# An encoder layer on one core: thirteen of the second matrix's sixteen pairs in seven products, the rest block by block, and the projection in one group

## The chip, the cores and the metric

The kernel runs on one core of a Trainium2 chip, as one program. The metric is the device time in microseconds (us) from the program's start to its end; lower is better. The kernel before takes 2405.2 us, the median of three runs that lie between 2405.2 and 2405.23 us.

## What is computed

One layer of an encoder is applied to two groups of tokens with the same weights: a prompt of 512 tokens and a sample of 1024 tokens, both with 1024 features. In short:

```
h = LN(x) * (1 + scale1) + shift1
x = LN1(alpha * x + gate1 * (m @ w_out))        # m: what two branches (convolution, long convolution) give
h = LN(x) * (1 + scale2) + shift2
f = square(relu(h @ mlp_w1 + mlp_b1))           # mlp_w1: 1024 x 4096
x = LN2(alpha * x + gate2 * (f @ mlp_w2 + mlp_b2))   # mlp_w2: 4096 x 1024
```

All of it is float32. The change concerns the sample's second half: the projection with `w_out`, and the two products of the MLP.

## The kernel before

**Products.** A float32 product is made of three matmuls of a reduced format (`mm3`, line 223): both operands are split into a high and a low part (`split`, line 201: ScalarE copies the high part, VectorE subtracts it from the source), and high by high, high by low and low by high are added up in PSUM. A weight tile of 128x512 therefore costs one DMA of 256 KB, one ScalarE copy and one VectorE subtraction before TensorE can use it.

**Order.** A tile scheduler lays down a fixed order of instructions for each engine; `soon(n)` moves what is issued within it n places of priority ahead. All DMAs stand in one queue, that of SP, and are issued in its order: a DMA whose buffer is not free yet holds up those behind it. All matmuls write PSUM tiles named `mm`, `fx` and `tr`, which hold 128x512 each; at most eight of them are in use.

**Projection (`w_out_ln1`, line 1018).** The sample's tokens are two blocks of 512, `tb` = 0 and 1, with four rows of 128 tokens each. A loop over four column quarters loads and splits four weight tiles (`wpiece`) and multiplies them for the rows of a group, in 128x256 products. For `tb` = 0 both pairs of rows form one group; for `tb` = 1 they are two groups one after the other, and each loads all 16 weight tiles anew. After a group's last quarter its rows are normalised (`ln1_pair`) in pieces that later steps pull from `self.todo`.

**First MLP matrix (`up_seven`, line 1263).** The 1024x1024 blocks of `h` and of each of 16 pairs of weight columns are multiplied with Strassen's scheme in Winograd's form: seven products in place of eight, of 12 matmuls each. Only some of the operands need the second token block. For the first `NE` = 12 pairs an early loop therefore does products 1 and 2 and parks what the main loop needs of them in DRAM (`d_xs`, `d_p`); `h2_second` (line 989), pulled one step at a time, makes the operands of the others. The main loop then does five products for an early pair and seven for a late one. Its results go to DRAM in seven slots of `d_p`, which hold the left operands of the second matrix: among them the sums `s1`, `s2`, `s4` and the difference `p21 - p11`, which only the seven products need.

**Second MLP matrix (`down_seven`, line 1396).** Again 16 pairs in seven products, here in four passes over the pairs, because the accumulators of one or two products fill PSUM: pass 1 (slots 0 and 1), pass 2 (slots 2 and 3), pass 3 (slots 4 and 5) and pass 4 (slot 6). Each step of a pass loads weights of 512 KB into a `pg` row (pass 2 one more of 256 KB into a `raw` tile, line 1464), forms weight sums on VectorE where the scheme needs them (`raw` and `pg`, line 1465 on), splits them into `wt` tiles, and loads and splits 512 KB of left operands (`load_p`, line 1427). A step is 24 matmuls of 128x512. The four double pairs that pass 4 does last are held back and done row by row (`held`), so that each row of `tb` = 0 can be finished by `ln2_end` (line 1534) while the next is multiplied. Those of `tb` = 1 are finished during pass 4 by `ln2_block` (line 1107).

Of the kernel before, what the change touches and what calls it, by code (L numbers as in the profile page):

```python
# [38 lines left out]
HD = 90  # L39
NE = 12  # L40
NL = 8
# [120 lines left out]
class Enc:  # L162
# [855 lines left out]
    def w_out_ln1(self, g):  # L1018
# [244 lines left out]
    def up_seven(self, g):  # L1263
# [4 lines left out]

        nc, v = self.nc, self.V
# [12 lines left out]
        for n in range(NE):  # L1282
# [25 lines left out]
        for n in range(NP):  # L1308
# [13 lines left out]
            def finish(last):  # L1322
# [7 lines left out]
                s4 = self.sg()  # L1330
                v.tensor_tensor(s4, t, s2, op=ALU.subtract)
                put(n - 1, 6, s4)
# [63 lines left out]
    def down_seven(self, g):  # L1396


        nc, v = self.nc, self.V
        w2 = self.a["mlp_w2"]  # L1400
        NP = 16
        row = lambda: self.pg(F32, (128, 2, 512))
# [4 lines left out]
        acc, st = {}, {}  # L1407
# [7 lines left out]
        def both(src, wt=True):  # L1415

            new = (lambda: self.p_wt.tile([128, 2, 512], F32R, tag="wt", name="wt")) if wt else self.pg
            h, l = new(), new()
            self.split(src, h, l)
            return h, l  # L1420

        def products(ps, p, w, j, i, first, last, more, blocks=range(4)):
            for m in blocks:
                k = slice(128 * m, 128 * m + 128)
                self.mm3(ps[m], p[0][:, j, k], p[1][:, j, k], w[0][:, i], w[1][:, i], first, last, skip_group_check=more)

        def load_p(src):
            t = row()
            nc.sync.dma_start(t, src)
            return both(t, False)  # L1430

        def half(t, tb, m, h):

            cs = slice(512 * h, 512 * h + 512)
            v.tensor_tensor(t, t, gate[:, cs], op=ALU.mult)
            v.tensor_tensor(acc[tb, m][:, cs], acc[tb, m][:, cs], t, op=ALU.add)
# [4 lines left out]
        for n in range(NP):  # L1441
            with self.soon(HD):
                t = row()
                nc.sync.dma_start(t, w2[2 * n:2 * n + 2, :, 0:512].rearrange("f p c -> p f c"))
                w = both(t)
                p = load_p(g.d_p[n, :, 0:2])
            products(b, p, w, 1, 1, n == 0, n == NP - 1, False)
            products(a, p, w, 0, 0, n == 0, n == NP - 1, False)
            if n % 2 and todo:
# [6 lines left out]
        for m in range(4):  # L1456
            v.tensor_tensor(ts[m], a[m], ts[m], op=ALU.add)
        t2 = {}
        for n in range(NP):
            with self.soon(HD):  # L1460
                t = row()
# [6 lines left out]
                v.tensor_tensor(u, u, t[:, 1], op=ALU.subtract)  # L1468
                v.tensor_tensor(s, t[:, 0], u, op=ALU.add)
                w6, w7 = self.piece(s), self.piece(u)  # L1470
                p = load_p(g.d_p[n, :, 2:4])
            products(b, p, (w7[:, 0:1], w7[:, 1:2]), 1, 0, n == 0, n == NP - 1, False)
            products(a, p, (w6[:, 0:1], w6[:, 1:2]), 0, 0, False, n == NP - 1, True)
            if n < 4:
                half(ts[n], 0, n, 0)
                st[n] = self.p_xt.tile([128, 2, 6], F32, tag="st2", name="st2")
                v.bn_stats(st[n][:, 0], acc[0, n][:, 0:512])
            yield 5.2
        m7, us = [], []
# [6 lines left out]
        for n in range(NP):  # L1486
            with self.soon(HD):
                t = row()
# [3 lines left out]
                w = both(t)  # L1492
# [9 lines left out]
        held = []  # L1502
        for n in range(0, NP, 2):
            late = n >= NP - NL
            with self.soon(HD):
                t = row()
                nc.sync.dma_start(t, w2[2 * n + 1:2 * n + 4:2, :, 512:1024].rearrange("f p c -> p f c"))
                w = both(t, n < NP - 2)
                p = load_p(g.d_p[n:n + 2, :, 6].rearrange("f p c -> p f c"))
            if n // 2 < 4:  # L1510
                m = n // 2
                half(m7[m], 1, m, 1)
                half(us[m], 1, m, 0)
                self.todo.append([self.ln2_block(g, 1, m, acc[1, m], lg, lb), 0])
            if late:
                held.append((p, w))
                continue
            for j in range(2):
                products(a, p, w, j, j, False, False, True)
            yield 5.2  # L1520
        for m in range(4):
            for k, (p, w) in enumerate(held):
                for j in range(2):
                    products(a, p, w, j, j, False, k == len(held) - 1 and j == 1, True, [m])
                yield 1.3
            t = self.so()
            v.tensor_tensor(t, a[m], gate[:, 512:1024], op=ALU.mult)
            s = acc[0, m]
            v.tensor_tensor(s[:, 512:1024], s[:, 512:1024], t, op=ALU.add)
            v.bn_stats(st[m][:, 1], s[:, 512:1024])  # L1530
            self.todo.append([self.ln2_end(g, m, s, st[m], lg, lb), 0])
        self.flush()

    def ln2_end(self, g, m, s, st, lg, lb):
        v = self.V
        mv = self.sm([128, 1, 2], tag="mv")
        v.bn_aggr(mv[:, 0], st)
        r = self.rstd(mv, 1)
        yield
        v.scalar_tensor_tensor(s, s, mv[:, 0, 0:1], lg, op0=ALU.subtract, op1=ALU.mult)  # L1540
        v.scalar_tensor_tensor(s, s, r[:, 0:1], lb, op0=ALU.mult, op1=ALU.add)
        yield
# [243 lines left out]
```

## Time and profile before

| what | value |
| --- | --- |
| median of three runs | 2405.2 us |
| the profiled execution's own time | 2408.34 us |
| its span | 2406.6 us |
| granted TensorE clock, mean | 0.988 |
| DMA, mean over the span | 175 GB/s |
| HBM read, written | 323.76 MB, 96.27 MB |

The profile shows one execution. Durations are those of its instructions; a stage's cost is read from a window of the trace: how long the stage lasts, how long each engine is busy in it, and what the engine that matters waits for. TensorE is named PE in the rows, VectorE DVE, ScalarE ACT, and the queue of SP is SPq. Instructions that a helper records all carry that helper's line (L145, L202), so tiles tell them apart better than lines do: in the second matrix `wt` is a split weight, `pg` a left operand or a row of the output, `raw` a weight as loaded; `st`, `mv` and `sm` belong to a normalisation.

### The profile page before, as it was taken

The numbers are of one execution on the slowest core, as the hardware profiler recorded it, in microseconds if no ns is written. First come the engines' busy times: TensorE is split into PE (matmuls) and PEld (weight loads), VectorE is DVE, ScalarE is ACT, GpSimd is POOL, SyncE is SP. The second block draws the span as 40 slices with busy tenths as digits, with TensorE's granted clock in tenths as the row PEclk, the third lists the DMA queues.
The fourth block names the chain that finished last, engine by engine and source line by source line (L and its number), as shares of the span: only waits on it lengthen the run. The fifth ranks groups of instructions, "written<-read, shape, count | busy, mean of one in ns | idle before, by whom it ended". The sixth has DMA issues, their size and how long they took to land.

```text
span 2406.6 us, 33012 instructions
## 1 busy us (share of the span) xinstructions
PE 2276.9 (95%) x11648; PEld 1878.9 (78%) x11648; DVE 1896.9 (79%) x3618; ACT 931.9 (39%) x1507; POOL 54.1 (2%) x149
## 2 busy tenths in 40 slices
PE   6999999999999999899999999997999999987995
PEld 3878777878878888888888887897777787866873
DVE  5988797877989989876988867749887785555678
ACT  3464422422222223365442353223664454423431
POOL 2110100000000000000000000000000000000000
PEclk9999999999999999999999999999999999999997
DMA  6555436663465566633433255545776666746543
GB/s 240 182 167 173 147 93 201 202 216 127 155 205 176 176 223 222 203 99 125 139 119 116 91 193 173 173 136 164 244 231 210 205 202 222 255 140 219 179 153 122
DMA packets 198250, 422.22 MB, mean 175 GB/s; under 512 B 22809, under 2 KB 33227, under 8 KB 197573
## 3 DMA queue, kind: packets, MB, share of 16 engines
q1 hardware_dynamic: 197253, 419.10, 52.7%
q8 instruction: 92, 1.51, 0.3%
q0 software_dynamic: 832, 1.02, 0.2%
q14 instruction: 73, 0.60, 0.1%
HBM read 323.76 MB, written 96.27 MB: 175 GB/s over the span
## 4 chain that ended last, share of the span: by engine, by line
PE 52%; DVE 13%; DMA 9%; issue 3%; ACT 2%; SPq 1%; DVEq 0%; ACTq 0%
PE mm L145 37%; PE fx L145 13%; DVE pg L145 3%; DVE wt L145 2%; PE tr L145 2%; DMA sg<-d_xs 1%; DVE fp L145 1%; DVE sg L145 1%; DVE st L145 1%; DMA sg<-ks 1%; DMA pg<-in_mlp_w_dram 1%; DMA raw<-in_w_out_dram 1%; DMA fp<-in_w_ada_dram 1%; DMA fp<-in_dec_s_dram 1%; DVE sm L145 1%
## 5 line engine op out<-in xcount | busy, mean ns | idle before, releaser
L145 PE MATMUL mm<-pg,wt 128*128 128x512 f32 (+1 forms) x4776 | 1139.9, 391 | 7.9 <-DVE xt L145 4.0
L145 PEld LDWEIGHTS mm<-pg,wt 128*128 128x128 f32 x4776 | 878.2, 189 | 196.9 <-issue 11.9
L145 PE MATMUL mm<-wt,pg 128*128 128x512 f32 (+1 forms) x2640 | 509.3, 348 | 22.8 <-DVE pg L145 14.1
L145 PEld LDWEIGHTS mm<-wt,pg 128*128 128x128 f32 x2640 | 422.3, 191 | 91.7 <-DVE pg L145 18.0
L202 ACT ACTIVATE wt<-raw 128x512 fp32r<-128x512 f32 x422 | 263.3, 629 | 455.4 <-PE mm L145 356.0
L145 DVE TENSOR_TENSOR wt<-raw,wt 128x512 fp32r<-128x512 f32 x422 | 284.6, 685 | 71.5 <-ACT wt L202 69.1
L145 DVE SCALAR_TENSOR_TENSOR cv<-cv,pp 128x512 f32<-128x512 f32 (+1 forms) x288 | 288.8, 1010 | 7.7 <-ACT cv L853 2.7
L145 PEld LDWEIGHTS fx<-fp,fft 128*128 128x128 f32 x1536 | 177.5, 192 | 22.7 <-issue 14.7
L145 PE MATMUL fx<-fp,fft 128*128 128x128 f32 x1536 | 184.2, 277 | 4.0 <-DVE fp L145 1.8
L145 DVE TENSOR_TENSOR fp<-fp 128x256 f32<-128x256 f32 (+2 forms) x328 | 145.1, 481 | 15.9 <-ACT fp L380 10.1
L145 DVE TENSOR_TENSOR sg<-fx,sg 128x512 f32<-128x512 f32 (+1 forms) x162 | 98.6, 630 | 47.7 <-PE fx L145 30.6
L145 PE MATMUL fx<-wt,pg 128*128 128x512 f32 x432 | 114.6, 403 | 19.7 <-ACT pg L202 18.4
L202 ACT ACTIVATE wt<-pg 128x1024 fp32r<-128x1024 f32 (+1 forms) x55 | 51.5, 936 | 193.4 <-DVE pg L145 84.7
L145 DVE TENSOR_TENSOR pg<-so,pg 128x512 fp32r<-128x512 f32 (+1 forms) x147 | 89.9, 617 | 37.7 <-ACT pg L202 26.4
L145 PEld LDWEIGHTS fx<-wt,pg 128*128 128x128 f32 x432 | 81.6, 192 | 42.7 <-ACT pg L202 22.6
L145 DVE TENSOR_TENSOR wt<-pg,wt 128x1024 fp32r<-128x1024 f32 (+1 forms) x55 | 58.8, 1068 | 68.5 <-ACT wt L202 68.4
L145 DVE TENSOR_TENSOR pg<-pg,pg 128x1024 fp32r<-128x1024 f32 (+1 forms) x74 | 88.9, 1220 | 10.0 <-DMA pg<-in_mlp_b_dram 6.6
L1260 ACT ACTIVATE so<-so,pp 128x512 f32<-128x512 f32 x60 | 43.2, 720 | 129.2 <-DVE so L145 128.9
L145 PE MATMUL fx<-pg,pg 128*128 128x512 f32 x384 | 92.8, 389 | 0.0
L202 ACT ACTIVATE pg<-so 128x512 fp32r<-128x512 f32 (+1 forms) x112 | 62.9, 567 | 68.9 <-DVE so L145 52.1
L145 DVE TENSOR_TENSOR sg<-sg 128x256 f32<-128x256 f32 (+2 forms) x187 | 82.2, 460 | 5.0 <-ACT sg L890 3.8
L145 PEld LDWEIGHTS fx<-pg,pg 128*128 128x128 f32 x384 | 72.0, 188 | 15.1 <-DVE so L145 0.2
(171 smaller groups left out, 2217.5 us busy)
## 6 DMA issues: line engine op xcount, KB each, us to landing
raw<-in_mlp_w_dram SPq DMA_DIRECT2D x188, 256.0 KB
raw<-in_w_in_dram SPq DMA_DIRECT2D x144, 256.0 KB
pg<-in_mlp_w_dram SPq DMA_DIRECT2D x56, 512.0 KB
pg<-d_p SPq DMA_DIRECT2D x56, 512.0 KB
fp<-in_w_ada_dram SPq DMA_DIRECT2D x48, 512.0 KB
raw<-in_w_out_dram SPq DMA_DIRECT2D x80, 256.0 KB
d_p<-so SPq DMA_DIRECT2D x64, 256.0 KB
d_g<-so SPq DMA_DIRECT2D x48, 256.0 KB
```

The lines of the kernel that those rows point to most:

```text
L145: return f(*args, **kw)
L202: self.nc.scalar.activation(hi, src, AF.Copy)
L1260: nc.scalar.activation(out, src, AF.Relu, bias=self.pp[:, C_B1 + f:C_B1 + f + 1], scale=1.0)
```

## The change

In the projection the rows of `tb` = 1 form one group, as those of `tb` = 0 do. In the first matrix 14 pairs are early instead of 12; the steps of `h2_second` are pulled from pair 8 on, behind a flush of the pending normalisation; and the last three pairs don't make `s1`, `s2`, `s4` and the difference. In the second matrix the first 13 pairs (`N7`) go through the seven products and the last three are multiplied block by block. Pass 3 becomes two passes of one product each (`single`), pass 4 a third of them. Weights are loaded in quarters of 256 KB, by turns into `raw` and `xr` tiles, and no longer in 512 KB rows of `pg`. For the last three pairs the weights are multiplied by the gate before they are split, and every row of 128 tokens gets its 36 matmuls directly and then its normalisation by `ln2_block`; `ln2_end` and `held` are gone.

```diff
-NE = 12
-NL = 8
+NE = 14
+N7 = 13
...
-            groups = [[0, 2]] if tb < g.nb - 1 else [[0], [2]]
+            groups = [[0, 2]] if g.nb > 1 else [[0], [2]]
...
-                if not self.todo:
+                if n >= NE - 6:
+                    if n == NE - 6 and k == 1:
+                        self.flush()
                     next(sums, None)
...
-            s1, s2 = self.sg(), self.sg()
-            v.tensor_tensor(s1, p21, p22, op=ALU.add)
-            put(n, 4, s1)
-            v.tensor_tensor(p21, p11, p21, op=ALU.subtract)
+            s2 = None
+            if n < N7:
+                s1, s2 = self.sg(), self.sg()
+                v.tensor_tensor(s1, p21, p22, op=ALU.add)
+                put(n, 4, s1)
+                v.tensor_tensor(p21, p11, p21, op=ALU.subtract)
+                v.tensor_tensor(s2, s1, p11, op=ALU.subtract)
+                put(n, 2, s2)
             put(n, 3, p21)
-            v.tensor_tensor(s2, s1, p11, op=ALU.subtract)
-            put(n, 2, s2)
...
+        def quarter(f, h):
+            t = self.xt("xr") if count[0] % 2 else self.p_raw.tile([128, 512], F32, tag="raw", name="raw")
+            count[0] += 1
+            nc.sync.dma_start(t, w2[f, :, 512 * h:512 * h + 512])
+            return t
...
-        for n in range(NP):
+        for n in range(N7):
             with self.soon(HD):
-                t = row()
-                nc.sync.dma_start(t, w2[2 * n].rearrange("p (h c) -> p h c", h=2))
-                u = self.p_raw.tile([128, 512], F32, tag="raw", name="raw")
-                nc.sync.dma_start(u, w2[2 * n + 1, :, 512:1024])
+                b11, b12, b22 = quarter(2 * n, 0), quarter(2 * n, 1), quarter(2 * n + 1, 1)
...
-        for n in range(NP):
-            with self.soon(HD):
-                t = row()
-                nc.sync.dma_start(t, w2[2 * n + 1].rearrange("p (h c) -> p h c", h=2))
-                s = t2[n // 2][:, n % 2:n % 2 + 1]
-                v.tensor_tensor(t, t, s.to_broadcast([128, 2, 512]), op=ALU.subtract)
-                w = both(t)
-                p = load_p(g.d_p[n, :, 4:6])
-            order = [(b, 1, 0), (a, 0, 1)]
-            for ps, j, i in order if n < NP - 1 else order[::-1]:
-                products(ps, p, w, j, i, False, n == NP - 1, True)
-            yield 5.2
+        def single(acc_ps, slot, row, h, minus, ops):
+            for n in range(0, N7, 2):
+                js = range(min(2, N7 - n))
+                with self.soon(HD):
+                    w = []
+                    for j in js:
+                        t = quarter(2 * (n + j) + row, h)
+                        if minus:
+                            v.tensor_tensor(t, t, t2[n // 2][:, j], op=ALU.subtract)
+                        w.append(self.piece(t))
...
+                for j in js:
+                    products(acc_ps, p, w[j], j, False, n + j == end, True)
+                some(ops, 2)
+                yield 5.2
...
+        yield from single(a, 4, 1, 1, True, iter(()))
         for m in range(4):
             v.tensor_tensor(m7[m], a[m], m7[m], op=ALU.add)
+        yield from single(b, 5, 1, 0, True, chain(*[half(m7[m], 1, m, 1) for m in range(4)]))
...
+        def rest_w(f, h, k):
+            t = quarter(f, h)
+            v.tensor_tensor(t, t, gate[:, 512 * h:512 * h + 512], op=ALU.mult)
+            wl[f, h] = w = self.pg(first=True) if k < 9 else self.p_wt.tile([128, 2, 512], F32R, tag="wt", name="wt")
+            self.split(t, w[:, 0], w[:, 1])
+
+        def rest_p(f, tb):
+            t = self.so()
+            nc.sync.dma_start(t, g.d_p[f // 2, :, (0, 1, 3, 5)[2 * tb + f % 2]])
+            x = pl[f, tb] = self.pg()
+            self.split(t, x[:, 0], x[:, 1])
...
+        last = single(a, 6, 1, 1, False, chain(*[half(us[m], 1, m, 0) for m in range(4)]))
+        for us_ in last:
+            with self.soon(HD):
+                some(prep, 2)
+            yield us_
...
+        for tb in (1, 0):
+            for m in range(4):
...
+                for h in range(2):
+                    ps = self.fx_ps() if m % 2 else self.mm_ps()
+                    for i, f in enumerate(fs):
+                        x, w = pl[f, tb], wl[f, h]
+                        self.mm3(ps, x[:, 0, k], x[:, 1, k], w[:, 0], w[:, 1], i == 0, i == len(fs) - 1)
+                    d = s[:, 512 * h:512 * h + 512]
+                    v.tensor_tensor(d, d, ps, op=ALU.add)
+                    yield 2.6
+                self.todo.append([self.ln2_block(g, tb, m, s, lg, lb), 0])
         self.flush()
```

How the change moves instructions is shown at two places. The first is SP's queue in pass 2 of the second matrix. In the kernel before, `pg2_19740`, `19787`, `19833` and `19880` are the 512 KB weight rows of the pass's pairs 0, 1, 2 and 3, `raw_19928`, `19971`, `20013` and `20056` the 256 KB quarters of pairs 4 to 7, and the loads from `d_p` the left operands of pairs 0 to 3:

```order
L1462 DMA pg2_19740<-in_mlp_w2_dram 128x1024
L1429 DMA pg2_19753<-d_p1_95 128x1024
L1462 DMA pg2_19787<-in_mlp_w2_dram 128x1024
L1429 DMA pg2_19799<-d_p1_95 128x1024
L1464 DMA raw_19928<-in_mlp_w2_dram 128x512
L1462 DMA pg2_19833<-in_mlp_w2_dram 128x1024
L1429 DMA pg2_19846<-d_p1_95 128x1024
L1464 DMA raw_19971<-in_mlp_w2_dram 128x512
L1462 DMA pg2_19880<-in_mlp_w2_dram 128x1024
L1429 DMA pg2_19892<-d_p1_95 128x1024
L1464 DMA raw_20013<-in_mlp_w2_dram 128x512
L1464 DMA raw_20056<-in_mlp_w2_dram 128x512
```

In the changed kernel's pass 2, `pg2_19702`, `19747` and `19793` are the left operands of pairs 2, 3 and 4; `raw_19869` and `raw_19873` with `xr_19871` are the three weight quarters of pair 6, `xr_19915`, `raw_19917` and `xr_19919` those of pair 7, and `raw_19960` and `raw_19964` belong to pair 8:

```order
L1418 DMA raw_19869<-in_mlp_w2_dram 128x512
L1418 DMA raw_19873<-in_mlp_w2_dram 128x512
L1429 DMA pg2_19702<-d_p1_95 128x1024
L1418 DMA xr_19871<-in_mlp_w2_dram 128x512
L1418 DMA xr_19915<-in_mlp_w2_dram 128x512
L1418 DMA xr_19919<-in_mlp_w2_dram 128x512
L1429 DMA pg2_19747<-d_p1_95 128x1024
L1418 DMA raw_19917<-in_mlp_w2_dram 128x512
L1418 DMA raw_19960<-in_mlp_w2_dram 128x512
L1429 DMA pg2_19793<-d_p1_95 128x1024
```

Before, a pair's 512 KB weight row stands right ahead of its left operands; now all of a pair's weight quarters stand some four pairs ahead of the left operands.

The second place is the end of VectorE's work, where `st` and `mv` are a row's statistics, `sm` the small steps to its scale, and the two SCALAR_TENSOR_TENSOR with `mv` and with `sm` its normalisation. Before, from the last row's statistics to the program's end:

```order
L145 BN_AGGR mv<-st_19924 128x2
L145 TENSOR_SCALAR sm<-sm 128x1
L145 SCALAR_TENSOR_TENSOR pg<-pg,mv,pg_19110 128x1024
L145 TENSOR_SCALAR sm<-sm 128x1 x5
L145 TENSOR_SCALAR sm<-mv 128x1
L145 SCALAR_TENSOR_TENSOR pg<-pg,sm,pg_19112 128x1024
L145 TENSOR_SCALAR sm<-sm 128x1 x8
L145 TENSOR_SCALAR sm<-mv 128x1
L145 SCALAR_TENSOR_TENSOR pg<-pg,sm,pg_19112 128x1024
L145 TENSOR_SCALAR sm<-sm 128x1 x8
L145 SCALAR_TENSOR_TENSOR pg<-pg,sm,pg_19112 128x1024
```

In the changed kernel, from the last product that is added (`fx`) to the end:

```order
L145 SCALAR_TENSOR_TENSOR pg<-pg,sm,pg_19024 128x1024
L145 TENSOR_TENSOR pg<-pg,fx 128x512
L145 BN_STATS st<-pg 128x6
L145 BN_AGGR mv<-st 128x2
L145 TENSOR_SCALAR sm<-mv 128x1
L145 SCALAR_TENSOR_TENSOR pg<-pg,mv,pg_19022 128x1024
L145 TENSOR_SCALAR sm<-sm 128x1 x8
L145 SCALAR_TENSOR_TENSOR pg<-pg,sm,pg_19024 128x1024
```

Before, three rows are still to be normalised when the last one's statistics are done; now the row ahead is finished before the last product is added.

More of the change, by code (lines that the diff above doesn't have):

```diff
@@ L1413, in base, with load_p, products, some @@
             v.scalar_tensor_tensor(s, s, ALPHA, gb, op0=ALU.mult, op1=ALU.add)
[L1415 to L1419, printed above, removed]
+        def load_p(src):
+            t = self.pg(F32, (128, 2, 512))
+            nc.sync.dma_start(t, src)
+            h, l = self.pg(), self.pg()
+            self.split(t, h, l)
             return h, l
-        def products(ps, p, w, j, i, first, last, more, blocks=range(4)):
-            for m in blocks:
+        def products(ps, p, w, j, first, last, more):
+            for m in range(4):
                 k = slice(128 * m, 128 * m + 128)
-                self.mm3(ps[m], p[0][:, j, k], p[1][:, j, k], w[0][:, i], w[1][:, i], first, last, skip_group_check=more)
-        def load_p(src):
-            t = row()
-            nc.sync.dma_start(t, src)
-            return both(t, False)
+                self.mm3(ps[m], p[0][:, j, k], p[1][:, j, k], w[:, 0], w[:, 1], first, last, skip_group_check=more)
         def half(t, tb, m, h):
             cs = slice(512 * h, 512 * h + 512)
-            v.tensor_tensor(t, t, gate[:, cs], op=ALU.mult)
-            v.tensor_tensor(acc[tb, m][:, cs], acc[tb, m][:, cs], t, op=ALU.add)
+            d = acc[tb, m][:, cs]
+            yield v.tensor_tensor(t, t, gate[:, cs], op=ALU.mult)
+            yield v.tensor_tensor(d, d, t, op=ALU.add)
+        def some(ops, n=1):
+            for _ in range(n):
+                next(ops, None)
+        def chain(*gens):
+            for x in gens:
+                yield from x
         a = [self.mm_ps() for _ in range(4)]
@@ L1440, in down_seven @@
         todo = [(tb, i) for tb in range(2) for i in range(4)]
-        for n in range(NP):
+        end = N7 - 1
+        for n in range(N7):
             with self.soon(HD):
-                t = row()
-                nc.sync.dma_start(t, w2[2 * n:2 * n + 2, :, 0:512].rearrange("f p c -> p f c"))
-                w = both(t)
+                w = [self.piece(quarter(2 * n + f, 0)) for f in range(2)]
                 p = load_p(g.d_p[n, :, 0:2])
-            products(b, p, w, 1, 1, n == 0, n == NP - 1, False)
-            products(a, p, w, 0, 0, n == 0, n == NP - 1, False)
-            if n % 2 and todo:
+            products(b, p, w[1], 1, n == 0, n == end, False)
+            products(a, p, w[0], 0, n == 0, n == end, False)
+            if n > 2 and todo:
                 base(*todo.pop(0))
@@ L1467, in down_seven @@
                 s = t2[n // 2][:, n % 2]
-                v.tensor_tensor(u, u, t[:, 1], op=ALU.subtract)
-                v.tensor_tensor(s, t[:, 0], u, op=ALU.add)
-                w6, w7 = self.piece(s), self.piece(u)
+                v.tensor_tensor(b12, b22, b12, op=ALU.subtract)
+                v.tensor_tensor(s, b11, b12, op=ALU.add)
+                w7, w6 = self.piece(b12), self.piece(s)
                 p = load_p(g.d_p[n, :, 2:4])
[L1472 to L1477, printed above, removed]
+            products(b, p, w7, 1, n == 0, n == end, False)
+            products(a, p, w6, 0, False, n == end, True)
+            some(ops)
             yield 5.2
+        some(ops, 9)
         m7, us = [], []
@@ L1521, in down_seven @@
-        for m in range(4):
[L1522 to L1531, printed above, removed]
@@ L1532, in down_seven @@
-        self.flush()
[L1534 to L1542, printed above, removed]
-        self.nc.sync.dma_start(g.out[128 * m:128 * m + 128, :], s)
-        yield
+        wl, pl = {}, {}
@@ new lines, in down_seven @@
+        with self.soon(HD):
+            for _ in prep:
+                pass
+            for k, (f, h) in enumerate(keys):
+                if k >= 9:
+                    rest_w(f, h, k)
+            for f in fs:
+                rest_p(f, 0)
+        c12 = []
+        for m in range(4):
+            c12.append(self.sg())
+            v.tensor_tensor(c12[m], a[m], gate[:, 512:1024], op=ALU.mult)
+        for tb in (1, 0):
+            for m in range(4):
+                s = acc[tb, m]
+                k = slice(128 * m, 128 * m + 128)
+                if tb == 0:
+                    v.tensor_tensor(s[:, 512:1024], s[:, 512:1024], c12[m], op=ALU.add)
+                for h in range(2):
[7 more added lines that the diff above has]
+                self.todo.append([self.ln2_block(g, tb, m, s, lg, lb), 0])
```

55 lines of the change are left out of this document (27 added, 28 removed).

## The prediction

> **What bounds the kernel now.** I began with the busy shares of the page, then cut the end of the program into its stages and read every engine in each, and only then looked at waits and at the chain.
>
> ```profile
> PE 2276.9 (95%) x11648; PEld 1878.9 (78%) x11648; DVE 1896.9 (79%) x3618; ACT 931.9 (39%) x1507; POOL 54.1 (2%) x149
> ```
>
> TensorE is busy 95% of the span, so a change gains where it takes matmuls away or where TensorE waits. The stages (start and end in us, stage length, busy time and count of each engine, granted clock, DMA share, GB/s):
>
> ```profile
> core 0: us, PE busy (x) PEld busy (x) DVE busy (x) ACT busy (x) POOL busy (x), PEclk, DMA share, GB/s
> 1634.00:1705.00 71.00, 55.73 (x418) 51.84 (x416) 67.53 (x172) 36.66 (x68) 0.00 (x0) 0.95 0.64 205
> 1705.00:1786.00 81.00, 80.60 (x374) 67.02 (x375) 73.13 (x153) 59.76 (x100) 0.00 (x0) 0.98 0.73 242
> 1786.00:1938.00 152.00, 144.30 (x616) 113.96 (x615) 111.14 (x180) 65.68 (x111) 0.00 (x0) 1.00 0.60 201
> 2015.00:2122.00 107.00, 103.24 (x453) 84.53 (x452) 55.97 (x54) 43.48 (x49) 0.00 (x0) 1.00 0.70 244
> 2122.00:2235.00 113.00, 94.09 (x375) 72.19 (x374) 70.01 (x94) 33.65 (x49) 0.00 (x0) 0.95 0.55 191
> 2235.00:2323.00 88.00, 86.78 (x383) 71.52 (x382) 54.92 (x48) 39.23 (x43) 0.00 (x0) 1.00 0.55 181
> 2323.00:2376.00 53.00, 45.38 (x187) 33.61 (x185) 52.43 (x96) 12.39 (x12) 0.00 (x0) 0.99 0.41 140
> 2376.00:2407.00 31.00, 8.05 (x22) 6.00 (x22) 23.79 (x60) 0.00 (x0) 0.00 (x0) 0.61 0.20 79
> ```
>
> In order these are the projection of the second token block, the early loop, the early pairs of the main loop, passes 1, 2, 3 and 4, and the end. TensorE is hardly idle in the early loop and pass 3, but 15 us in the projection, 8 in the main loop, 19 in pass 2, 8 in pass 4, and nearly all of the end. In the projection VectorE is busy 67.5 of 71 us, in pass 4 52.4 of 53: there it sets the pace. In pass 2 it is busy 70 of 113, so there it is something else.
>
> The price of a matmul comes from pass 1 in the chain (start, length, what):
>
> ```profile
> 2049.20 2.72 PE mm L145 x12
> ```
>
> Twelve fed matmuls of 128x512 take 2.72 us, 0.2267 each.
>
> **Matmuls.** Of 16 pairs in seven products of 12 matmuls per pair and four rows (84 x 16 = 1344) 13 stay (1092), and the last three become eight blocks of 2 x 18 (288): 1380, 36 more. **+8.2 us** (36 x 0.2267).
>
> **Projection and early loop.** The groups of the first window for TensorE and VectorE, and a fed stretch of 256-wide matmuls from the chain:
>
> ```profile
> L145 PE MATMUL mm<-wt,pg 128*128 128x256 f32 x382 | 53.4, 294 | 12.2 <-DVE pg L145 10.4 <-DVE wt L145 1.5 <-ACT wt L202 0.2
> L145 PE MATMUL tr<-ident,pg 128*128 128x128 f32 x32 | 7.0, 291 | 0.4 <-ACT so L971 0.3
> L145 DVE TENSOR_TENSOR wt<-raw,wt 128x512 fp32r<-128x512 f32 x31 | 20.8, 685 | 1.5 <-ACT wt L202 1.1 <-issue 0.3
> 1683.33 1.08 PE mm L145 x9
> ```
>
> 382 products at 0.12 are 45.8 us, the transposes 7.0 and four wide matmuls 0.9: 53.7, so about 17 of 71 us are lost, and VectorE ends most of those waits. One group of rows takes away 16 weight tiles: 16 x 0.685 = 11.0 us of VectorE. Two more early pairs bring 48 matmuls (10.9 us) out of the main loop and, with two weight tiles and one sum each, 6 x 0.685 = 4.1 us of VectorE. Over both windows VectorE then needs 67.5 + 73.1 - 11.0 + 4.1 = 133.7 us and TensorE 53.7 + 80.6 + 10.9 = 145.2; the same work takes 71 + 81 + 10.9 = 162.9 now. If TensorE becomes the bound without a gap, 17.7 are gained; if the stage stays VectorE's and only its 11.0 go, 11. At 92% VectorE will still hold TensorE up here and there, for the normalisation and the operand sums now come in two bunches, ahead of pair 8 and behind it. I take **-14**.
>
> **Main loop.** An early pair is 60 matmuls, 13.6 us, but the chain steps by more:
>
> ```profile
> 1793.90 5.36 DMA sg<-d_xs
> 1800.09 3.03 PE mm L145 x12
> 1877.47 3.07 PE mm L145 x12
> ```
>
> Between the last two stand five pairs: 77.4 / 5 = 15.5, 1.9 lost each, behind a load of the parked product. Two more early pairs: 0 to +3.8. **+3**, as those rows are the same operation. The sums left out for three pairs stand in the late part, beside 84 matmuls a pair, and gain nothing.
>
> **Start of pass 1.** 3.8 us idle in its window (107.0 - 103.2); the order of left operands and output rows there changes, so 0 to -3.8. **-2**.
>
> **Pass 2.** 16 steps of 24 matmuls are 87.0 us; the window has 113: 26 lost, 1.63 a step. The waits of the window (total, times, longest) and the chain:
>
> ```profile
> DVE raw L145 <- DMA pg<-in_mlp_w_dram: 25.1, 9, 3.2
> PE fx L145 <- ACT pg L202: 17.1, 9, 2.8
> 2144.33 4.09 DMA pg<-in_mlp_w_dram
> 2152.34 4.02 DMA pg<-in_mlp_w_dram
> 2168.38 6.63 DMA pg<-d_p
> ```
>
> Every 8 us a 512 KB weight row lands on the chain and VectorE waits for it. It is asked for too late: its `pg` buffer comes free late and it stands right ahead of its own left operands, as the change's section shows. DMA is idle 45% of the window. Afterwards the quarters have buffers of their own and stand some four pairs ahead. A step moves the same bytes (three quarters and 512 KB, 1.31 MB in 5.44 us: 241 GB/s). If the waits stay, 13 x 1.63 = 21 are lost; if it runs like pass 3 (88 for 87.0), one. I take 5, near pass 3, since VectorE also has pass 1's results to add at its start. **-21**, bounds -5 to -25.
>
> That 256 KB transfers carry this rate is seen in the early loop, whose loads are nearly all of that size (its DMA view):
>
> ```profile
> GB/s 374 397 134 164 225 185 74 185 251 329 132 409 413 184 261 289 16 259 129 129 299 219 241 81 336 276 293 213 231 296 238 214 324 251 129 171 367 361 340 268
> DMA packets 10245, 19.62 MB, mean 242 GB/s; under 512 B 1140, under 2 KB 1140, under 8 KB 10239
> raw<-in_mlp_w_dram SPq DMA_DIRECT2D x16, 256.0 KB
> ```
>
> 242 GB/s as a mean and slices of 413. The Trainium skill ("DMA: Bandwidth & Descriptors", section "Bandwidth") speaks against the smaller loads: it asks for transfers of at least 1 MiB, and the fit in its section "Anatomy of one DMA", made on another issue path, gives an estimated 2.6 us for 256 KB. If the transfers of a step took turns at that, the step would be about 11 us and the sum some 70 us worse; the slices above speak against turns.
>
> **The three single-product passes.** Pass 3 loses 1 us now. Pass 4 runs from the end of pass 3's last matmuls to the end of the last matmul:
>
> ```profile
> 2319.89 2.96 PE mm L145 x13
> 2375.90 8.15 PE L145 MATMUL mm<-pg,pg 128*128 128x512 f32 x22 [3.88 <-DVE pg L145]
> L145 DVE TENSOR_TENSOR pg<-pg,pg 128x1024 fp32r<-128x1024 f32 x16 | 19.5, 1218 | 0.0
> ```
>
> 2322.9 to 2384.1 is 61.2 us for 192 matmuls of 43.5: 17.7 lost. Afterwards the normalisations leave this place for the block part, but VectorE gets other work. Over the three single passes (468 matmuls, 106.1 us): 26 weight subtractions, 39 low parts, 16 half-row steps, 8 sums, 4 gate products, 24 steps on the rest's weights, 12 on its left operands and 3 odd ones, 132 x 0.685 = 90.4, and 18 low parts of 128x1024, 21.9: 112 against 106. Back to back, as they stand in the chain near the end of pass 3, the same operations take 0.60 and 1.13:
>
> ```profile
> 2325.36 1.13 DVE wt L145
> 2326.50 0.60 DVE xt L145
> ```
>
> That would make 100. So VectorE is close to the bound, and I let each part lose 4 to 5 us: pass 3 **+3** (0 to +8), pass 4 against the last pass **-12.7** (-5 to -17.7).
>
> **End.** From the last matmul at 2384.05 to 2406.6 are 22.5 us, in which VectorE has four rows to finish. The rows for one (timeline):
>
> ```profile
> 2389.79 0.68 DVE L145 TENSOR_TENSOR pg<-pg,so 128x512 f32<-128x512 f32 x1
> 2391.65 0.68 DVE L145 BATCH_NORM_STATS2 st<-pg 128x6 f32<-128x512 f32 x1
> 2392.37 0.21 DVE L145 BATCH_NORM_AGGREGATE mv<-st 128x2 f32<-128x12 f32 x1
> 2399.63 2.01 DVE L145 TENSOR_SCALAR sm<-sm 128x1 int32<-128x1 int32 x8
> 2401.68 1.28 DVE L145 SCALAR_TENSOR_TENSOR pg<-pg,sm,pg 128x1024 f32<-128x1024 f32 x1
> ```
>
> The last step ends at 2402.96, the output's store 3.6 later. Afterwards one row is left: 0.68 + 0.68 + 0.21 + 1.28 + 2.15 + 1.28 + 3.6 = 9.9. A block's 36 matmuls are 8.16 us, its VectorE work two or three sums, two statistics and this chain: 7.7 to 8.4, so half a microsecond of lag may be left. **-12** (-8 to -12.6).
>
> **The sum.** 8.2 - 14 + 3 - 2 - 21 + 3 - 12.7 - 12 = -47.5. Against the profiled execution's own 2408.3 (its span 2406.6 and 1.7 around it) that is 2360.8; the median lies 3.1 below that execution, so **2358 us**.
>
> **Rivals.** *VectorE binds.* Passes 3 and 4 and the blocks need 100% of it, so its bursts show as waits: some 12 us more, 2370. For: 112 against 106. Against: the blocks, 65 us, can take some of it. Chance 0.13.
> *The projection's wait moves.* The normalisation of four rows now waits for the last quarter, the operand sums wait for it, and the main loop starts late: the 14 are not gained, 2372. For: VectorE at 92%. Chance 0.07.
> *The change does not do what it says*, for a quarter stuck in SP's queue holds up the left operands behind it: pass 2 keeps its 1.63 a step, 2374. Against: quarters stand four pairs ahead. Chance 0.05.
> *Slower*: that same wait in all five passes of seven products, because the queue is one and each step now has twice as many loads with buffers that must come free. The terms outside the passes sum to -16.8, and the losses in passes 2 to 4 now are 26 + 1 + 17.7 = 44.7. At x lost per 24 matmuls, 1092 / 24 = 45.5 steps give -61.5 + 45.5x: from 1.35 us it is slower, from 1.46 by over 0.2%; with pass 2's own 1.63 it is +13, 2418. Against: passes 1 and 3 run on the same queue nearly without loss. Chance 0.06. The skill's rule on transfer size would lead here.
>
> **Numbers.** My forecast has 0.69. Within it the bounds of the terms go 21 us down if all are met, 19 as I take it (2339), and about as far up; the middle rivals reach 2374 and, two at once, 2385. So 2339 to 2385, with the slower rival and part of the combinations outside. Within 0.2%, which is about what a measurement of this kernel can tell from no change, I put 0.03, for three middle rivals together; slower 0.06; faster 0.91.
>
> **What would show it.** Projection and early loop together at about 149 us for the work of 163; pass 2 in 76 us, with no 512 KB weight row on the chain; the three single passes in some 115; an unbroken 65 us of blocks; 10 us from the last matmul to the end. It would be wrong if TensorE waited for `raw` or `xr` loads step after step, if VectorE stood at 100% over the single passes, or if the main loop began late, behind the operand sums.

## The result and the profile after

The changed kernel takes 2346.7 us (median of four runs, 2344.9 to 2351.8) against 2405.2 us before: a ratio of 0.9757, 95% interval 0.974 to 0.9774. Forecast were 2358 us and a range of 2339 to 2385. The profiled execution has a span of 2350.0 us, 56.6 less than the one before.

The stages of the changed kernel, in the same view as before (start and end, length, busy time and count of each engine, granted clock, DMA share, GB/s):

```profile
core 0: us, PE busy (x) PEld busy (x) DVE busy (x) ACT busy (x) POOL busy (x), PEclk, DMA share, GB/s
1634.00:1690.00 56.00, 53.35 (x426) 51.00 (x425) 51.57 (x137) 29.37 (x52) 0.00 (x0) 1.00 0.58 191
1690.00:1777.00 87.00, 82.30 (x389) 68.31 (x387) 76.14 (x164) 61.83 (x103) 0.00 (x0) 1.00 0.66 222
1777.00:1957.00 180.00, 170.74 (x721) 134.73 (x722) 132.13 (x214) 76.25 (x129) 0.00 (x0) 0.99 0.62 205
2024.00:2095.00 71.00, 71.00 (x311) 58.71 (x310) 45.11 (x54) 30.84 (x42) 0.00 (x0) 0.99 0.78 257
2095.00:2166.00 71.00, 71.00 (x315) 58.82 (x314) 56.40 (x79) 32.62 (x48) 0.00 (x0) 1.00 0.67 219
2166.00:2201.00 35.00, 35.00 (x155) 28.71 (x155) 22.07 (x31) 17.54 (x26) 0.00 (x0) 1.00 0.59 191
2201.00:2237.00 36.00, 36.00 (x161) 29.81 (x160) 33.29 (x49) 17.18 (x26) 0.00 (x0) 1.00 0.72 231
2237.00:2272.00 35.00, 35.00 (x156) 29.01 (x155) 32.02 (x51) 19.16 (x32) 0.00 (x0) 1.00 0.54 174
2272.00:2340.00 68.00, 68.00 (x301) 56.03 (x299) 55.16 (x123) 0.00 (x0) 0.00 (x0) 1.00 0.12 47
2340.00:2350.00 10.00, 0.05 (x1) 0.00 (x0) 5.89 (x14) 0.00 (x0) 0.00 (x0) 0.66 0.26 105
```

They are the projection of the second token block, the early loop, the early pairs of the main loop, pass 1, pass 2, the two halves of pass 3, the last pass, the blocks and the end. From 2024 us on TensorE is busy in every microsecond until its last matmul, and the end behind it is 10 us long instead of 22.5.

To put one number on each stage, I took for every matmul how much later the next one started than the median for its shape (0.227 us for 128x512, 0.120 for 128x256, 0.112 for 128x128), and summed this per stage. The end is the time behind the last matmul.

| stage | lost before, us | lost after, us | difference | forecast |
| --- | --- | --- | --- | --- |
| projection, early loop, step to the main loop | 25.5 | 12.1 | -13.4 | -14 |
| main loop | 13.2 | 17.0 | +3.8 | +3 |
| start of pass 1, pass 1 | 4.6 | 4.8 | +0.2 | -2 |
| pass 2 | 28.2 | 0.0 | -28.2 | -21 |
| pass 3 | 1.5 | 0.2 | -1.3 | +3 |
| pass 4 / last pass and blocks | 14.0 | 0.0 | -14.0 | -12.7 |
| end | 22.5 | 9.95 | -12.6 | -12 |
| 36 matmuls more | | | +8.2 | +8.2 |
| sum | | | -57.3 | -47.5 |

The sum stands within a microsecond of the spans' difference. Two places were better than forecast: pass 2 by 7 us, and the single-product passes, which lose 0.2 us in all, by 6.

The first row of the table holds a gain and a new loss. Of its 12.1 us after, 4.4 are lost in one wait at the step into the main loop, which the kernel before doesn't have (TensorE around 1771 us; total, times, longest):

```profile
PE fx L145 <- ACT pg L202: 4.3, 1, 4.3
```

The chain runs over VectorE there, from 1767.8 to 1776.3 us. So projection and early loop themselves gained some 18 us, and part of that was lost again where the main loop begins. The same 4.4 us are lost in the profile of every kernel below that is derived from the changed one; no run tried to remove it.

The end, in the timeline of the changed kernel, is the one row that was forecast at 9.9 us:

```profile
2340.09 0.69 DVE L145 TENSOR_TENSOR pg<-pg,fx 128x512 f32<-128x512 f32 x1 [0.94 <-PE fx L145]
2340.81 0.69 DVE L145 BATCH_NORM_STATS2 st<-pg 128x6 f32<-128x512 f32 x1
2343.04 2.01 DVE L145 TENSOR_SCALAR sm<-sm 128x1 int32<-128x1 int32 x8
2345.09 1.28 DVE L145 SCALAR_TENSOR_TENSOR pg<-pg,sm,pg 128x1024 f32<-128x1024 f32 x1
```

VectorE even waits 0.94 us for the last product, so the blocks' normalisations don't pile up behind TensorE.

What the prediction had not looked at is SP's own row. In pass 2 of the kernel before, the timeline shows when SP issued its loads (start, length, what):

```profile
2144.33 0.42 SPq L1462 DMA_DIRECT2D pg<-in_mlp_w_dram  x1
2144.85 0.38 SPq L1429 DMA_DIRECT2D pg<-d_p  x1
2151.96 0.33 SPq L1464 DMA_DIRECT2D raw<-in_mlp_w_dram  x1
2152.34 0.42 SPq L1462 DMA_DIRECT2D pg<-in_mlp_w_dram  x1
2152.82 0.42 SPq L1429 DMA_DIRECT2D pg<-d_p  x1
2159.91 0.33 SPq L1464 DMA_DIRECT2D raw<-in_mlp_w_dram  x1
2160.28 0.43 SPq L1462 DMA_DIRECT2D pg<-in_mlp_w_dram  x1
```

and the waits of that window put a name to it (total, times, longest):

```profile
SPq L1464 <- DVE wt L145: 79.9, 12, 12.5
```

SP stands 79.9 of 113 us in front of L1464, the load of a 256 KB quarter, until VectorE has split an earlier quarter and its `raw` tile is free. The 512 KB row of a pair needed much sooner stands right behind it. The row lands 4 us later, VectorE splits it, that frees the next `raw` tile, and so on: one step every 8 us, where TensorE needs 5.44. The `pg` buffer isn't what the row waits for.

A wait of SP alone costs nothing. In the changed kernel's pass 2 SP still waits 53.5 of 71 us in front of weight quarters, for the most part like this:

```profile
SPq L1418 <- DVE wt L145: 29.3, 15, 4.5
```

There TensorE is never idle, because what stands behind in the queue comes in time all the same.

### The profile page after: what moved, and what is told of

Same layout as the page of the kernel before. It is cut to its first block, busy times and chain, and to the rows that moved or that the text cites. A ratio compares the mean times of both kernels' runs of the same rounds, so it can differ in the third digit from the quotient of the medians.

```text
span 2350.0 us, 33224 instructions
## 1 busy us (share of the span) xinstructions
PE 2267.9 (97%) x11684; PEld 1882.4 (80%) x11684; DVE 1890.1 (80%) x3662; ACT 920.5 (39%) x1521; POOL 54.3 (2%) x149
## 4 chain that ended last, share of the span: by engine, by line
PE 79%; DVE 9%; DMA 8%; ACT 2%; issue 2%; SPq 1%; DVEq 0%; ACTq 0%
PE mm L145 57%; PE fx L145 19%; PE tr L145 3%; DVE sg L145 2%; DVE pg L145 2%; DVE wt L145 1%; DMA fp<-in_dec_s_dram 1%; DMA sg<-d_xs 1%; DMA fp<-in_w_ada_dram 1%; DVE st L145 1%; DVE fp L145 1%; DMA sg<-in_ffn_w_dram 1%; DMA sg<-ks 1%; DMA raw<-in_w_out_dram 1%; DVE xt L145 1%
## 5 line engine op out<-in xcount | busy, mean ns | idle before, releaser
L145 PE MATMUL mm<-wt,pg 128*128 128x512 f32 (+1 forms) x2556 | 480.8, 344 | 9.5 <-DVE wt L145 5.0
L145 PEld LDWEIGHTS mm<-wt,pg 128*128 128x128 f32 x2556 | 404.8, 190 | 68.6 <-DVE wt L145 6.8
L145 DVE TENSOR_TENSOR pg<-so,pg 128x512 fp32r<-128x512 f32 (+1 forms) x162 | 99.6, 623 | 38.3 <-ACT pg L202 26.9
L145 PE MATMUL fx<-pg,pg 128*128 128x512 f32 x492 | 120.7, 394 | 7.2 <-ACT pg L202 4.3
L145 PEld LDWEIGHTS fx<-pg,pg 128*128 128x128 f32 x492 | 93.5, 190 | 27.5 <-ACT pg L202 4.7
L202 ACT ACTIVATE pg<-so 128x512 fp32r<-128x512 f32 (+1 forms) x127 | 72.1, 575 | 73.9 <-DVE so L145 52.0
L145 PE MATMUL fx<-wt,pg 128*128 128x512 f32 x387 | 95.5, 389 | 0.0
L145 PE MATMUL mm<-pg,pg 128*128 128x512 f32 x300 | 73.9, 396 | 5.5 <-DVE xt L145 5.5
L380 ACT ACTIVATE fp<-fx 128x512 f32<-128x512 f32 x48 | 28.7, 598 | 120.6 <-PE fx L145 110.4
L145 DVE TENSOR_TENSOR pg<-pg,pg 128x1024 fp32r<-128x1024 f32 (+1 forms) x45 | 55.0, 1221 | 24.4 <-ACT pg L202 19.6
```

Source lines behind the costliest of these rows:

```text
L145: return f(*args, **kw)
L202: self.nc.scalar.activation(hi, src, AF.Copy)
L380: nc.scalar.activation(outs[-1][:, 4 * (pr % 2):4 * (pr % 2) + 4].rearrange("p (j w) c -> p j w c", j=2), ps, AF.Copy)
```

## The experiments

Twelve kernels ran, in three groups of four; the kernel before ran again in each group, the changed kernel again in the third. Times are medians. Runs of the changed kernel and of those derived from it scatter by 7 to 11 us, and in the profiles most of that scatter lies ahead of what the change touches: TensorE's last long wait ahead of the projection, here in the kernel before and the changed one,

```profile
1479.84 5.32 PE L145 MATMUL mm<-wt,pg 128*128 128x512 f32 x15 [3.04 <-DVE pg L145]
```

```profile
1480.92 2.12 PE L145 MATMUL mm<-wt,pg 128*128 128x512 f32 x8 [2.82 <-DVE pg L145]
```

ends anywhere from 1473 to 1482 us. The last column of the table therefore counts from there to the end: 926.7 us before, 869.1 after.

| kernel | us | ratio to before, 95% | from the landmark, us |
| --- | --- | --- | --- |
| before, pass 2 in quarters | 2378.5 | 0.9899 (0.9879 to 0.9919) | 899.4 |
| before, quarter in a `pg` buffer | 2382.1 | 0.9911 (0.9887 to 0.9935) | 904.8 |
| before, quarter in `raw` and `xr` | 2394.9 | 0.9958 (0.9943 to 0.9972) | 911.0 |
| after, projection in two groups | 2367.6 | 0.9845 (0.9825 to 0.9865) | 883.2 |
| after, 12 early pairs | 2347.2 | 0.9760 (0.9738 to 0.9781) | 863.1 |
| after, 14 pairs in seven products | 2349.9 | 0.9769 (0.9749 to 0.9789) | 871.1 |
| after, extra VectorE work | 2349.5 | 0.9772 (0.9751 to 0.9794) | 871.2 |
| after, bias product later | 2349.0 | 0.9772 (0.9743 to 0.9801) | 869.4 |
| after, unaltered | 2347.7 | 0.9776 (0.9761 to 0.9790) | 868.1 |
| after, parked product in `pg` | 2332.2 | 0.9718 (0.9703 to 0.9732) | 855.3 |
| the same with 12 early pairs | 2334.4 | 0.9726 (0.9709 to 0.9743) | 856.3 |
| after, pass 2 with 512 KB rows | 2359.4 | 0.9826 (0.9806 to 0.9846) | 880.7 |

### Pass 2: which part of the loads it is

The first three put one piece of the change's loads into the kernel before.

**Quarters alone.** Pass 2's weights come in three quarters by turns into `raw` and `xr`; nothing else changes.

```diff
-                t = row()
-                nc.sync.dma_start(t, w2[2 * n].rearrange("p (h c) -> p h c", h=2))
-                u = self.p_raw.tile([128, 512], F32, tag="raw", name="raw")
-                nc.sync.dma_start(u, w2[2 * n + 1, :, 512:1024])
+                t0, t1, u = quarter(2 * n, 0), quarter(2 * n, 1), quarter(2 * n + 1, 1)
...
-                v.tensor_tensor(u, u, t[:, 1], op=ALU.subtract)
-                v.tensor_tensor(s, t[:, 0], u, op=ALU.add)
+                v.tensor_tensor(u, u, t1, op=ALU.subtract)
+                v.tensor_tensor(s, t0, u, op=ALU.add)
```

(`quarter` is the change's function.)

> The kernel before, with only pass 2's weights loaded as three 256 KB quarters by turns into raw and xr tiles. Pass 2 lost 26 us there (113 for 87.0), in steps of 8 us: SP waits in front of the load of a 256 KB quarter until VectorE has split an earlier pair's quarter and so freed the raw tile, and the 512 KB row of a later pair stands behind it in SP's queue. Queue theory: with the quarters this loop is gone, pass 2 takes 88 to 92 us, the whole kernel 2380 to 2384 us. Rival (the change's gain in pass 2 comes from having three pairs fewer and less VectorE work there, not from the loads): pass 2 stays above 105 us, the whole above 2397.

**Quarter in a `pg` buffer.** The 512 KB row stays; only the quarter no longer uses a `raw` tile.

```diff
-                u = self.p_raw.tile([128, 512], F32, tag="raw", name="raw")
+                u = self.pg(F32, (128, 2, 512))[:, 0]
                 nc.sync.dma_start(u, w2[2 * n + 1, :, 512:1024])
```

> The kernel before, with pass 2's 256 KB quarter loaded into a pg buffer in place of a raw tile; the 512 KB row stays as it is, and a step now takes five pg buffers instead of four. Queue theory: no load waits for a split of raw any more, so the 8 us step goes: pass 2 in 88 to 95 us, the whole 2380 to 2388 us. Rival (the prediction's words: the row's pg buffer comes free late): with more pg buffers used per step it gets worse, pass 2 at 113 us or more, the whole 2405 or more. Rival (512 KB is too large a transfer to land in time): no change, 2403 to 2407.

**Eight buffers instead of four.**

```diff
-                u = self.p_raw.tile([128, 512], F32, tag="raw", name="raw")
+                u = self.xt("xr") if n % 2 else self.p_raw.tile([128, 512], F32, tag="raw", name="raw")
                 nc.sync.dma_start(u, w2[2 * n + 1, :, 512:1024])
```

> The kernel before, with pass 2's 256 KB quarter by turns in raw and xr tiles: eight buffers instead of four. In SP's queue the quarter of pair n+8 now stands ahead of the row of pair n+2, as that of pair n+4 did, and still waits for the split of pair n or n+1. Queue theory: no change, 2402 to 2407 us and steps of 8 us. Rival (too few raw buffers): pass 2 falls to 88 to 95 us, the whole to 2380 to 2388.

Pass 2's length can be read from ScalarE's copies of the `fx` accumulators ahead of it and behind it. Before:

```profile
2118.82 1.57 ACT L1455 ACTIVATE sg<-fx 128x512 f32<-128x512 f32 x3 [10.68 <-PE fx L145]
2234.10 1.57 ACT L1482 ACTIVATE sg<-fx 128x512 f32<-128x512 f32 x3 [5.48 <-PE fx L145]
```

with quarters:

```profile
2123.00 1.57 ACT L1462 ACTIVATE sg<-fx 128x512 f32<-128x512 f32 x3 [0.89 <-PE fx L145]
2209.52 1.96 ACT L1486 ACTIVATE sg<-fx 128x512 f32<-128x512 f32 x3 [0.43 <-PE fx L145]
```

with the quarter in `pg`:

```profile
2112.49 1.57 ACT L1455 ACTIVATE sg<-fx 128x512 f32<-128x512 f32 x3 [10.68 <-PE fx L145]
2205.70 1.58 ACT L1482 ACTIVATE sg<-fx 128x512 f32<-128x512 f32 x3 [9.17 <-PE fx L145]
```

and with eight buffers:

```profile
2113.98 1.58 ACT L1455 ACTIVATE sg<-fx 128x512 f32<-128x512 f32 x3 [10.68 <-PE fx L145]
2218.57 1.58 ACT L1482 ACTIVATE sg<-fx 128x512 f32<-128x512 f32 x3 [6.40 <-PE fx L145]
```

That is 115.3 us before, 86.5 with quarters, 93.2 with the quarter in `pg`, 104.6 with eight buffers; 16 steps of 24 fed matmuls are 87. The quarters alone bring the whole of pass 2's gain in a kernel with 16 pairs, so the smaller number of pairs isn't needed for it. Nor is the row's size or its `pg` buffer at fault: the second kernel keeps the row, uses more `pg` buffers per step, and is still nearly rid of the wait. (In it the row's place in SP's queue changed together with the quarter's pool; no run changed the order alone.) The third was expected to change nothing and gained more than a third, 10.7 of 28.8 us. Its timeline says why:

```profile
2154.88 0.33 SPq L1464 DMA_DIRECT2D xr<-in_mlp_w_dram  x1
2155.26 0.43 SPq L1462 DMA_DIRECT2D pg<-in_mlp_w_dram  x1
2162.92 0.33 SPq L1464 DMA_DIRECT2D raw<-in_mlp_w_dram  x1
2163.30 0.42 SPq L1462 DMA_DIRECT2D pg<-in_mlp_w_dram  x1
2170.47 0.33 SPq L1464 DMA_DIRECT2D xr<-in_mlp_w_dram  x1
2170.85 0.42 SPq L1462 DMA_DIRECT2D pg<-in_mlp_w_dram  x1
2171.80 0.42 SPq L1462 DMA_DIRECT2D pg<-in_mlp_w_dram  x1
2172.97 0.50 SPq L1462 DMA_DIRECT2D pg<-in_mlp_w_dram  x1
```

The step of 8 us goes on for as long as quarters are left to load. With eight buffers each stands eight pairs ahead, so the sixteenth is issued at 2170.47, half way through the pass; from there the next rows follow each other a microsecond apart. More buffers did not break the loop, they let it run out earlier.

**The reverse, in the changed kernel.** Two of the three quarters become a 512 KB row again.

```diff
-                b11, b12, b22 = quarter(2 * n, 0), quarter(2 * n, 1), quarter(2 * n + 1, 1)
+                row = self.pg(F32, (128, 2, 512))
+                nc.sync.dma_start(row, w2[2 * n].rearrange("p (h c) -> p h c", h=2))
+                b11, b12 = row[:, 0], row[:, 1]
+                b22 = quarter(2 * n + 1, 1)
...
-                v.tensor_tensor(b12, b22, b12, op=ALU.subtract)
-                v.tensor_tensor(s, b11, b12, op=ALU.add)
-                w7, w6 = self.piece(b12), self.piece(s)
+                v.tensor_tensor(b22, b22, b12, op=ALU.subtract)
+                v.tensor_tensor(s, b11, b22, op=ALU.add)
+                w7, w6 = self.piece(b22), self.piece(s)
```

With it the difference is formed in the quarter's own tile, as in the kernel before, so that this tile comes free only after its split.

> The changed kernel, with pass 2's first two weight quarters loaded as one 512 KB row into a pg buffer, as before; the third quarter stays in raw and xr by turns. In SP's queue a quarter of pair n+8, later one of the next pass, again stands ahead of a row of pair n+1 or n+2 and waits for a split. Queue theory: the steps of 8 us are back over most of the 13 pairs, pass 2 takes 90 to 105 us in place of 71, the whole is 15 to 30 us slower. Rival (with three pairs fewer and eight buffers the wait is gone in any case): within 4 us.

It is 11.7 us slower than the unaltered kernel of its group. The waits of pass 2 and its issues:

```profile
SPq L1418 <- DVE wt L145: 73.8, 20, 6.1
2144.57 0.33 SPq L1418 DMA_DIRECT2D raw<-in_mlp_w_dram  x1
2144.99 0.38 SPq L1478 DMA_DIRECT2D pg<-in_mlp_w_dram  x1
2150.68 0.33 SPq L1418 DMA_DIRECT2D xr<-in_mlp_w_dram  x1
2151.10 0.38 SPq L1478 DMA_DIRECT2D pg<-in_mlp_w_dram  x1
```

The loop is back, at 6.1 to 7.3 us a step and not 8, so pass 2 loses 10 us and the whole less than the 15 to 30 expected. Why a step is shorter here was not tried.

### Projection and early loop

> The changed kernel, with the projection's second token block in two groups again (16 weight tiles more). My term for projection and early loop together was -14 us. If the one group is what brings it: slower by 9 to 15 us, 2356 to 2362, with TensorE idle over 10 us in the projection again. Rival (the order of the normalisation and of the operand sums brings it): within 4 us of the changed kernel.

```diff
-            groups = [[0, 2]] if g.nb > 1 else [[0], [2]]
+            groups = [[0, 2]] if tb < g.nb - 1 else [[0], [2]]
```

From the landmark it is 14.1 us slower, and the waits of before are there again (TensorE in the 73 us from 1627):

```profile
PE mm L145 <- DVE pg L145: 10.2, 4, 4.9
PE mm L145 <- DVE wt L145: 3.5, 2, 2.6
```

The one group brings this stage's gain. (Its median lies some 20 us above the changed kernel's of other groups, more than the 9 to 15 expected; the profiled execution was the fastest of four, and how much of the rest is the scatter ahead of the landmark isn't known.)

> The changed kernel with 12 early pairs again (operand sums pulled from pair 6 on). Against the changed kernel: in the main loop two waits of 1.2 to 1.9 us less, but 10.9 us of TensorE work less in the early loop to lie beside VectorE's work there. If that work is needed as cover: projection, early loop and the gap behind it lose 20 us or more (12 in the changed kernel), the whole is 4 to 9 us slower. Rival (VectorE keeps up with 12 pairs as well): 2 to 4 us faster.

With 12 early pairs the profile is 6 us shorter from the landmark, the median the same. By the measure of the first table, projection and early loop lose 12.6 us up to the same wait ahead of the main loop, where the changed kernel loses 12.1, and the main loop some 13 instead of 17. So the two pairs more were not needed as cover, and in the main loop they cost some 4 us; whether the whole is slower for them, the equal medians can't say.

### The blocks and the single-product passes

> The changed kernel with 14 pairs in seven products and two block by block: 12 matmuls less (-2.7 us), and a row's block part 24 matmuls, 5.4 us, where VectorE was busy 55.2 us over the eight rows, 6.9 a row. Cover theory (the block part is there to lay TensorE work beside the normalisations): the block part becomes VectorE's, 55 to 62 us in place of 43.5, so the whole is 8 to 15 us slower. Rival (only the matmuls count): 2 to 3 us faster.

Within the scatter of the changed kernel, 2.0 us slower from the landmark. TensorE waits for nothing in the blocks here either, but its last matmul and VectorE's last step stand further apart (timeline):

```profile
2325.66 1.75 PE L145 MATMUL fx<-pg,pg 128*128 128x512 f32 x7
2339.34 1.28 DVE L145 SCALAR_TENSOR_TENSOR pg<-pg,sm,pg 128x1024 f32<-128x1024 f32 x1
```

From 2327.4 to the span's end at 2344.4 are 17.0 us against 9.95: VectorE falls 7 us behind over eight rows, and the 12 matmuls saved give 2.7 back. The cover theory's sign is right and its size too large: VectorE needs 6.3 us a row (5.4 + 7/8) and not 6.9.

```diff
                 for j in js:
                     products(acc_ps, p, w[j], j, False, n + j == end, True)
+                for _ in range(EXTRA):
+                    v.bn_stats(self.p_xt.tile([128, 6], F32, tag="extra", name="extra"), acc[0, 0][:, 0:512])
                 some(ops, 2)
```

> The changed kernel with one more VectorE operation (statistics of a half row that nothing uses, 0.6 to 0.69 us) in each step of the three single-product passes: 21, some 14 us. The prediction held VectorE to be at the bound there (112 us against 106) and gave these parts 8 us of loss; the profile after shows 87.4 us busy of 106 and no loss. Slack theory: 0 to 3 us slower. Bound theory: 10 to 14 us slower.

This run did not test what it was made for. The statistics depend on nothing late, and the scheduler laid all 21 into pass 2:

```profile
L146 DVE BATCH_NORM_STATS2 extra<-pg x21: 676/684/695, 2112.6 to 2148.8; 128x6 f32<-128x512 f32 x21
```

What it shows is that pass 2 takes them for little: VectorE is busy 66.3 us of 71 there instead of 56.4, TensorE then waits 3.5 us at the start of pass 3 for a copied accumulator, and the whole is 2.1 us longer from the landmark. That the single-product passes are not VectorE's is read from the profile alone: 22.1, 33.3 and 32.0 us busy of 35, 36 and 35.

### The start of pass 1

```diff
         gb = self.bcast_row(self.a["mlp_b2"])
-        v.tensor_tensor(gb, gb, gate, op=ALU.mult)
...
+            if n == 2:
+                v.tensor_tensor(gb, gb, gate, op=ALU.mult)
```

> The changed kernel with the product of bias and gate (VectorE, waits 4.8 us for the bias row) moved behind the third step of pass 1. TensorE waits 2.9 us there for a VectorE sum that stands behind that product; the prediction's -2 for this place did not come (4.6 us lost before, 4.8 after). If that product is what holds it: the gap at the start of pass 1 falls below 1 us and the whole by 2 to 4 us. Rival (the sum waits for the first weights of pass 1 anyway): no change within 1.5 us.

No change. The gap there is shorter in that profile (1.8 us for 3.3), but it is 1.7 to 2.7 in other profiles that keep the product in its place, so the edit isn't the cause. The chain of this run speaks for the rival: the first weights of pass 1 land there at 2016.6 us, 4.55 us after their issue, and lead over a split and a left operand to the sum that TensorE waits for until 2019.05.

### A version that beats both

The queue theory has a second place. In the main loop of the changed kernel, SP issues the load of a pair's parked product right behind a store that waits for VectorE (timeline):

```profile
1793.49 0.33 SPq L1271 DMA_DIRECT2D d_p<-sg  x1
1793.87 0.42 SPq L1344 DMA_DIRECT2D sg<-d_xs  x1
```

and the product is needed when it lands. The edit takes another buffer and a higher priority (no run separates the two), and with them the scheduler places the load ahead of these stores:

```diff
-                x = self.sg()
-                with self.soon(40):
+                x = self.pg(F32, (128, 2, 512), True)[:, 0]
+                with self.soon(90):
                     nc.sync.dma_start(x, g.d_xs[n])
```

> The changed kernel, with the main loop's parked product loaded into a pg buffer in place of one of the six sg buffers. In SP's queue its load then stands some ten places earlier, ahead of the stores of the pair before, each of which waits for VectorE's or ScalarE's result. Queue theory: the 4 to 5 us landing leaves the chain, the main loop loses 9 to 12 us in place of 16.5, and 5 to 8 us are gained. Rival (TensorE would wait for the next VectorE sum anyway): within 2 us of the changed kernel.

> The same with 12 early pairs. With 12 pairs the profile was 6 us shorter from the landmark than with 14, though the median was the same. If the two add up: 8 to 14 us faster than the changed kernel, 2333 to 2340. If the 12 pairs' gain was scatter: as the run with 14 pairs within 2 us.

2332.2 us against 2347.7 for the unaltered kernel on the same chip, their intervals against before apart: 15.5 us (12.8 from the landmark), twice what was expected. The issue and the main loop's window of this kernel:

```profile
1797.50 0.40 SPq L1344 DMA_DIRECT2D pg<-d_xs  x1
1799.85 0.33 SPq L1271 DMA_DIRECT2D d_p<-sg  x1
1776.00:1957.00 181.00, 181.00 (x792) 146.67 (x791) 148.21 (x241) 87.43 (x146) 0.00 (x0) 1.00 0.68 228
```

The load now stands ahead of the pair's `sg` stores, and TensorE is busy 181.0 of 181 us, where it was idle 9.3 of 180. A second wait has gone with it: the changed kernel's TensorE waited 12 times, 9.1 us in all, for the VectorE sum (`xt`) that frees the accumulator,

```profile
PE mm L145 <- DVE xt L145: 9.1, 12, 1.0
```

and with the load early no TensorE wait is left in that window. I take it that these sums were late because the parked product, which they add, was; no run separates the two. With 12 early pairs there is nothing further to gain (2334.4): without this wait 12 and 14 early pairs cost the same within what these runs can tell.

## Why the prediction was right, point by point

**Right in its mechanism and size:** the matmuls; the projection's one group (-14 forecast, -13.4 by the table, 14.1 by the run that undoes it); the main loop's price for two more early pairs (+3, measured +3.8, and some 4 by the run with 12); the end (9.9 us forecast, 9.95 measured). Of projection and early loop, the rival in which the main loop starts late came true in part: some 18 us were gained in the projection and the early loop, and the wait ahead of the main loop took 4.4 of them.

**Pass 2, right in place and sign, wrong in cause.** The prediction said of the row that "its `pg` buffer comes free late and it stands right ahead of its own left operands". The runs showed that the `pg` buffer is free, and that what holds the row is the load ahead of it in SP's queue, which waits for a `raw` tile. The forecast came out because the change removes that too, which was luck as far as the stated cause goes. Its size was too small: the term kept 5 us of loss, near pass 3 and for VectorE's sums at the start of the pass, and there was none; the other 2 are the loss before, 28.2 us by the table's measure and 26 by the prediction's. The rival in which a stuck quarter holds up the left operands had the right mechanism, in the wrong kernel.

**Single-product passes, a term mis-sized.** The prediction put 112 us of VectorE work into 106 and gave pass 3 and the last pass 8 us of loss. The profile has 87.4 us of it there and a loss of 0.2, for two reasons. There are 131 operations and not 150, because the scheduler had laid the others into pass 2 (56.4 busy of 71) and the blocks. And most stand back to back: at the 0.60 and 1.13 us that the prediction had read for that, but did not use in its sum, 115 operations of 128x512 and 16 of 128x1024 come to 87.1. From forecast to result, pass 2 and these passes are 7.2 + 4.3 + 1.3 us better and the end 0.6, and 3.6 are worse elsewhere: 9.8 in all.

**Start of pass 1, not shown.** -2 was taken from a change of order. In the profile after TensorE loses as much there as before (4.8 us for 4.6), but in a second profile of the changed kernel it loses 3.2 and in other kernels with the same order 1.9 to 4.1, so the term is within the scatter.

**The range.** The prediction says that the bounds of its terms reach about as far up as the 21 us down. As they stand they add up to 38 us upwards, 16 of them pass 2's; the upper end of 2385 is 27 above the forecast.

**Transfer size.** Pass 1 moved 257 GB/s and pass 2 219 with 256 KB weight loads beside 512 KB left operands, and from 2024 us on TensorE waited in neither. The Trainium skill ("DMA: Bandwidth & Descriptors", section "Bandwidth") asks for at least 1 MiB per transfer; in this trace the smaller loads cost nothing, and whether larger ones would move more no run shows.

## What to carry to other kernels

Where one queue issues all loads, look first at what the queue itself waits for and at what stands behind that wait; a load that comes late may have had its buffer all along. More buffers for the blocking load need not help much; another pool for one of the two did here, and each time the load's place in the queue changed with it. Work that only the end needs, such as a row's normalisation, can lie beside TensorE's when the last products are ordered row by row, with at least as much TensorE time per row as VectorE needs: at 8.2 us a row VectorE kept up here, at 5.4 it fell 7 us behind over eight rows.

## What was not expected of the hardware

In pass 2 and in the projection, where TensorE waited in short bursts, the granted clock was 0.95; with the waits gone it is 1.00 in the same stages, so a removed wait gave back more than its idle time. In pass 2 TensorE was idle 19 us and lost 28.2; some 7 of the 9 between are 40 matmuls that started 0.43 us apart instead of 0.227, behind the three longest of its waits (2.3 to 2.8 us). And executions of the same instructions ahead of the projection differ by up to 9 us, more than several of the edits tried here are worth.
